# A hybrid HGRN2 / RWKV-7 backbone: small matmuls recorded in groups, HGRN2's key folded into its logarithms, and the mixers' weight remainders on VectorE

## The chip, the cores and the metric

The kernel runs on one core of one Trainium2 chip. The metric is the device time of one launch in microseconds; the kernel before took 4508.4 us (median of three runs, 4477.64 to 4508.42).

The names of a profile: PE is TensorE's matmuls and PEld its weight loads, DVE is VectorE, ACT is ScalarE, POOL is GpSimd, SP issues the DMAs.

## The reference

Four layers, each over 512 tokens (256 of context, 256 latent) of 1024 channels; in the last layer only the latent half is read out. A layer has a token mixer and a SwiGLU channel mixer. The token mixer feeds one input projection to two recurrences, merges them with sigmoid gates and projects out:

```python
p = modulate(rms_norm(x, g), shift, scale) @ w_in[l]          # 1024 -> 6528 columns
hg, rw, gates = split(p)
# HGRN2, per head of 128: forward and reversed, summed
S_t = diag(f_t) S_{t-1} + k_t v_t^T;   o_t = S_t^T q_t        # k = (1 - lb) sigmoid(-f)
# RWKV-7, per head of 64: forward and reversed, summed
S = S * w_t + (-S kk_t) b_t^T + v_t k_t^T;   y_t = S r_t
m = sigmoid(g_hg) * (o_hg @ proj_a) + sigmoid(g_rw) * (o_rw @ proj_b)
x = x + gate * rms_norm(m @ w_out)
x = x + gate * rms_norm((silu(h @ w1a) * (h @ w1b)) @ w2)     # 2816 hidden
```

## The kernel before

Everything is kept channel-major: 128 channels in the partitions, 512 tokens along the free axis. Each dense projection is done in three TensorE passes of rounded operands. A weight block of 512 rows by 128 columns comes by DMA into `wr`; ScalarE rounds it into `wh`; a subtraction gives the remainder `wl` (`load_split`); and a matmul each is made of `wh` with the rounded activations, `wh` with their remainder, and `wl` with the rounded ones (`mm3`). In a profile these are the `p_ps<-...` matmuls, 128 rows by 128 columns by 512 tokens. There are 102 such weight blocks in a layer's input projection.

The remainder's engine comes from `plan.lo(i)` and the table `LO`: entries 0 and 2 are for the input projections (layers 0 to 2, and the last), 1 and 3 for everything behind. A 1 stands for `plan.any`, VectorE or GpSimd, whichever the planner finds free first; a 0 for GpSimd.

The small matmuls are plain fp32, and each appears in a profile as two instructions:

- RWKV-7 works on four pairs of heads per layer. A pair holds head h = 0 in partitions 0 to 63 and head h = 1 in 64 to 127 (`hd[h]`). `rw_pair` builds the chunk products: `ZA` (64 x 64 blocks, `s_ps<-XS,BK` and `s_ps<-XS,X8b`, 64*64) and `SC` (64 rows to 128 columns, the same names, 64*128). `rw_solve` inverts the triangular blocks, mostly on VectorE. `rw_chain` goes through the eight chunks of 64 tokens and, at four of them, writes outputs (`c_ps<-SC,UV` with 128 rows, and `c_ps<-XS,S` with 64 rows in the half of the head).
- HGRN2 works on four heads per layer. `hg_head` makes the scores of a head level by level: at level h = 1, 2, 4, ..., 64 ScalarE takes exponentials of running sums of log forget gates (`PF`, `SB`, `SF`, `PB`) into X and Y, VectorE multiplies X by q and Y by the keys kf and kb, TensorE multiplies them (`score`, `g_ps<-hX,hY`), and GpSimd doubles the span of the sums.

These streams are recorded side by side, together with the projections of the gates. A list schedule (`Plan.schedule`) then gives each engine one fixed order: of what could start, what the longest chain of work hangs on. Its costs are a table in `Plan.cost`. `together()` records several instructions of an engine as one piece that nothing can come between. The engines run their lists in order; a wait at the head of a list holds all behind it. PSUM has four banks for projections (`p_ps`), two for `s_ps`, and one each for `c_ps` and `g_ps`.

The names are those of the line that issues everything (L341); a group is told by its tiles.

Of the kernel before, what the change touches and what calls it, by code (L numbers as in the profile page):

```python
# [10 lines left out]
F32R = mybir.dt.float32r  # L11
# [40 lines left out]
      ("X4c", 2, 1), ("SS", 2, 1), ("PF", 1, 2), ("SB", 1, 2), ("kf", 1, 2), ("kb", 1, 2))  # L52
# [9 lines left out]
LO = (1, 0, 1, 1)  # L62
ADA = (0.96, 0.58)
WRB, WSB = 4, 3
B2 = ("PF", "SB", "kf", "kb", "hq")
# [18 lines left out]
class Node:  # L84
    """One instruction, or several of an engine in a row, with what it waits for."""
# [7 lines left out]
class Plan:  # L93
    """Takes down the kernel's instructions, and emits them in the order of a list schedule: each engine runs, of what
    could start, what the longest chain of work hangs on."""
# [3 lines left out]
    def __init__(self, nc, tc):  # L99
        self.tc, self.nodes, self.tiles, self.tags, self.gang, self.kind = tc, [], {}, {}, None, None  # L100
        self.eng = dict(zip(self.ENG, (nc.tensor, nc.scalar, nc.vector, nc.gpsimd, nc.sync)))
# [22 lines left out]
    def region(a):  # L124
        """Partitions and elements that an access pattern spans."""
# [13 lines left out]
    def together(self):  # L139
        """The instructions recorded in this context, all of one engine, stay one after another."""  # L140
        @contextmanager
        def group():
            self.gang = -1
            yield
            self.gang = None
        return group()

    def add(self, engs, name, args, kw):
# [27 lines left out]
        costs = [self.cost(e, name, out, args, kw) for e in engs]  # L176
# [19 lines left out]
    def cost(eng, name, out, args, kw):  # L196
        """Nanoseconds that an instruction holds its engine."""
# [154 lines left out]
def body(ctx, tc, xT, cc, ada_w, w_in, rw_lo, rw_g2, proj_a, proj_b, w_out, ffn_w1, ffn_w2,  # L352
# [122 lines left out]
    def load_split(src, k0, nk, c0, ncol, place=None):  # L475
        """Weight rows k0*128.. and columns c0.. as its rounded part and the rest."""
# [24 lines left out]
    def psum2(w, src, hi, lo, rg=slice(0, T), tag="s"):  # L501
        """PSUM tile with w^T src for w of zeros and ones, src going in two parts."""
# [7 lines left out]
    def spots(tile):  # L510
        """Places for the split weights of one output tile in [P, 4, T]."""
# [7 lines left out]
    def proj(src, nk, c0, xh, xl, t0, place=None):  # L519
        """PSUM tile with W[:, c0:c0+128]^T x for tokens t0.., with a place for the weights stream by stream."""  # L520
# [24 lines left out]
    def norms(xs, t0, post=None, pre=None):  # L545
        """x += G * rms_norm(y), and then h = rms_norm(x) * A + B per channel and stream, split in two parts."""
# [79 lines left out]
    def ada_put(pm, b, n, ps):  # L626
        """Sums of n blocks of columns from b on, each stream's in 128 / 2 n rows, put channel-major in md."""
# [12 lines left out]
    def ada_first(l, pm):  # L640
        """The first four blocks of 512 columns of silu(c) @ ada_w[l], each in a quarter of the rows."""
# [14 lines left out]
    def ada_pair(l, pm, b):  # L656
        """Blocks b and b + 1, the products summed over the rows of each partition first."""
# [22 lines left out]
    def ada_finish(pm, i):  # L680
        """Scale, shift and gate of sub-layer i // 3 with the norm weights in."""
# [31 lines left out]
    def sigm(o, src, nb, t):  # L713
        """o = sigmoid(src - nb) by exp and ln; t is all of o."""
# [5 lines left out]
    def shifted(ps, j, lmu, t0, tag):  # L720
        """pf = p + mu (shift(p) - p) of projection tile j."""
# [20 lines left out]
    def layer(l, pm, xs, xd, hh, hl):  # L742
# [32 lines left out]
        def stacked(src, tags):  # L775
            """Per direction src's rounded part and the rest, in the two halves of the rows."""
# [33 lines left out]
        def rw_pair(p):  # L810
# [103 lines left out]
            if EA[last]:  # L914
                for d in range(2):
                    for h in range(2):
                        hs = hd[h]
                        ps = sps()
                        for i in range(NCH):
# [595 lines left out]
```

## Time and profile before

| | before |
|---|---|
| median of the runs | 4508.4 us (4477.64 to 4508.42) |
| span of the profiled execution | 4491.0 us |
| input projection and mixers of layers 0, 1, 2, 3 | about 630, 666, 665, 633 us |
| merge and channel mixer of layers 0, 1, 2, 3 | about 549, 505, 507, 276 us |

The profiled execution's span lies between the runs, 17.4 us below their median. The stages are told apart by their weight loads: the first loads of `w_in` lead the mixers, the first of `proj_a` the merge.

### The profile page before, as it was taken

To read this page: it belongs to the slowest core of one execution; us is meant where nothing else is said; L and a number is where in the kernel's file an instruction comes from. 1 tells how busy PE (TensorE), PEld (TensorE's weight loads), DVE (VectorE), ACT (ScalarE), POOL (GpSimd) and SP (SyncE) were. 2 spreads that over 40 slices of the span, in tenths; PEclk is the share of its full clock that TensorE was granted. 3 is DMA by queue.
4 is the path that set the end of the run, shared out by engine and by line. 5 is a ranking of instruction groups with operands and counts; after the bars stand their busy time and mean duration, and the time that the engine had idled before them with its cause. 6 is when DMAs were issued, how large, how long until landed. Compare 5 with 4: busy or idle time off the path is not lost. (4 is left out here: it accounts for less than half of the span.)

```text
span 4491.0 us, 72501 instructions
## 1 busy us (share of the span) xinstructions
PE 4151.3 (92%) x26290; PEld 3248.2 (72%) x26290; DVE 3314.2 (74%) x5772; ACT 2161.3 (48%) x4458; POOL 2318.9 (52%) x2121
## 2 busy tenths in 40 slices
PE   7999998899999999989999999999899989888998
PEld 5676776677777767778777676677777766667888
DVE  5988878977388898676627988876754487887665
ACT  4554653433255565534434554554433354554564
POOL 2464654465445456454654554554555535455542
PEclk8998899999998998899999998899999988887999
DMA  4211127455421111354433211116444421111555
GB/s 151 59 46 36 51 88 227 140 166 158 134 73 57 49 44 46 125 173 125 139 114 122 63 49 41 46 56 205 122 146 124 137 67 43 41 44 39 159 151 162
DMA packets 661415, 451.08 MB, mean 100 GB/s; under 512 B 28224, under 2 KB 584256, under 8 KB 661056
## 3 DMA queue, kind: packets, MB, share of 16 engines
q1 hardware_dynamic: 661056, 446.44, 33.1%
q8 instruction: 207, 3.39, 0.3%
q14 instruction: 152, 1.25, 0.1%
HBM read 416.98 MB, written 29.36 MB: 99 GB/s over the span
## 5 line engine op out<-in xcount | busy, mean ns | idle before, releaser
L341 POOL TENSOR_TENSOR wl<-wr,wh 128x512 fp32r<-128x512 f32 x726 | 1017.5, 1404 | 1034.3 <-ACT wh L341 705.9
L341 PE MATMUL p_ps<-hh,wh 128*128 128x512 f32 (+1 forms) x2784 | 1073.7, 398 | 30.2 <-ACT wh L341 15.8
L341 PE MATMUL p_ps<-hh,wl 128*128 128x512 f32 (+1 forms) x2784 | 1053.1, 397 | 30.9 <-POOL wl L341 21.4
L341 PE MATMUL p_ps<-hl,wh 128*128 128x512 f32 (+1 forms) x2784 | 1060.0, 394 | 0.0
L341 ACT ACTIVATE wh<-wr 128x512 fp32r<-128x512 f32 x986 | 610.0, 621 | 844.3 <-PE p_ps L341 678.8
L341 PEld LDWEIGHTS p_ps<-hh,wl 128*128 128x128 f32 x2784 | 544.5, 198 | 157.8 <-POOL wl L341 46.9
L341 PEld LDWEIGHTS p_ps<-hh,wh 128*128 128x128 f32 x2784 | 541.9, 197 | 145.2 <-ACT wh L341 26.9
L341 PEld LDWEIGHTS p_ps<-hl,wh 128*128 128x128 f32 x2784 | 543.4, 198 | 97.0 <-issue 9.2
L341 POOL TENSOR_SCALAR fn<-fn 128x512 f32<-128x512 f32 (+1 forms) x152 | 230.9, 1519 | 177.4 <-ACT fn L341 168.8
L341 DVE TENSOR_TENSOR fn<-fn,p_ps 128x512 f32<-128x512 f32 (+1 forms) x208 | 127.1, 614 | 219.9 <-ACT fn L341 129.0
L341 POOL TENSOR_SCALAR S0P<-S,pcs 128x64 f32<-128x64 f32 x192 | 156.7, 829 | 222.0 <-DVE S L341 221.2
L341 DVE TENSOR_TENSOR wl<-wr,wh 128x512 fp32r<-128x512 f32 x260 | 186.9, 723 | 101.1 <-ACT wh L341 59.7
L341 DVE TENSOR_TENSOR XS<-XS,S 64x30 f32<-64x30 f32 (+14 forms) x480 | 214.0, 446 | 10.8
L341 ACT ACTIVATE fn<-fn 128x512 f32<-128x512 f32 (+1 forms) x304 | 174.3, 574 | 89.7 <-POOL fn L341 84.9
L341 DVE TENSOR_TENSOR S<-XS 64x30 f32<-64x30 f32 (+14 forms) x480 | 207.3, 432 | 10.8
L341 PE MATMUL s_ps<-XS,X8b 64*64 64x64 f32 (+2 forms) x1024 | 147.2, 298 | 23.2 <-ACT X8a L341 14.5
L341 POOL TENSOR_TENSOR SF<-SF,PF 128x256 f32<-128x256 f32 x112 | 90.9, 812 | 139.0 <-ACT hY L341 138.2
L341 PEld LDWEIGHTS s_ps<-XS,X8b 64*128 64x128 f32 (+1 forms) x1024 | 118.9, 196 | 55.2 <-ACT X8a L341 24.1
L341 PE MATMUL s_ps<-XS,BK 64*64 64x64 f32 (+2 forms) x1024 | 139.2, 275 | 13.3 <-DVE XS L341 12.6
L341 PEld LDWEIGHTS s_ps<-XS,BK 64*128 64x128 f32 (+1 forms) x1024 | 107.9, 175 | 58.9 <-issue 37.1
L341 DVE SCALAR_TENSOR_TENSOR UV<-c_ps,pcs,S0P 64x64 f32<-64x64 f32 x384 | 108.6, 283 | 56.1 <-PE c_ps L341 45.6
L341 PE MATMUL p_ps<-SC,wh 128*128 128x512 f32 (+1 forms) x440 | 143.4, 363 | 2.4 <-ACT SC L341 2.2
(525 smaller groups left out, 9554.7 us busy)
## 6 DMA issues: line engine op xcount, KB each, us to landing
wr<-ffn_w SPq DMA_DIRECT2D x512, 256.0 KB, 3.0
wr<-w_in SPq DMA_DIRECT2D x408, 256.0 KB, 2.9
hq<-ada_w SPq DMA_DIRECT2D x242, 256.0 KB, 2.9
PB<-ada_w SPq DMA_DIRECT2D x110, 256.0 KB, 3.0
wr<-w_out SPq DMA_DIRECT2D x64, 256.0 KB, 3.0
gts<-fn SPq DMA_DIRECT2D x48, 256.0 KB, 3.0
wr<-proj_a SPq DMA_DIRECT2D x32, 256.0 KB, 4.5
wr<-proj_b SPq DMA_DIRECT2D x32, 256.0 KB, 3.8
```

What stands on the lines that cost most here:

```text
L341: getattr(self.eng[self.on[i]], name)(*args, **kw)
```

## The change

Three things are changed, none of which alters the amount of dense work.

**Small matmuls.** The `ZA` and `SC` products take two PSUM banks at a time, one for each head, and alternate between the heads, recorded with `together`. The outputs of the chain are sorted so that first all products with `UV` come, then all with the state `S`, alternating between the heads. The other small products of the chain are put in `together` as they are. The planner gets a smaller cost for such groups (`share`).

**HGRN2.** The exponential of the key's logarithm is no longer taken ahead; the logarithm is the start value of `SF` and `PB`. `SB` and `PF` lie in one tile `HA`, `SF` and `PB` in `HB`, and an access pattern (`both`) takes the two halves that a level needs in one instruction.

**Remainders.** `LO` goes from (1, 0, 1, 1) to (2, 0, 2, 1), where 2 is VectorE alone.

```diff
-LO = (1, 0, 1, 1)
+LO = (2, 0, 2, 1)
...
-        return self.any if LO[i] else self.pool
+        return self.vec if LO[i] == 2 else self.any if LO[i] else self.pool
...
+    def together(self, share=1.0):
         @contextmanager
         def group():
-            self.gang = -1
+            self.gang, self.share = -1, share
             yield
-            self.gang = None
+            self.gang, self.share = None, 1.0
...
-        costs = [self.cost(e, name, out, args, kw) for e in engs]
+        costs = [self.cost(e, name, out, args, kw) * self.share for e in engs]
...
+                    pz = [sps().rearrange("p (s c) -> p s c", s=4) for _ in range(2)]
+                    with plan.together(0.55):
+                        for i in range(4):
+                            for h in range(2):
+                                pe.matmul(pz[h][:, i, 0:w], BK[hd[h], s4 + i, :, :], ar[hd[h], s4 + i, 0:w // C, :],
+                                          start=True, stop=True)
                     for h in range(2):
-                        hs = hd[h]
-                        ps = sps()
-                        psv = ps.rearrange("p (s c) -> p s c", s=4)
-                        for i in range(4):
-                            pe.matmul(psv[:, i, 0:w], BK[hs, s4 + i, :, :], ar[hs, s4 + i, 0:w // C, :], start=True,
-                                      stop=True)
...
+                    steps += [(0, i, 0, n), (0, i, 1, sb)] + [(1, i, 0, n)] * (n > 0) + [(1, i, 1, sb)] * (sb > 0)
+                steps.sort()
+                fin = {i: x for x in steps for i in (x[1],)}
+                with plan.together(0.75):
+                    for x in steps:
+                        st_, i, d, n = x
+                        for h in range(2):
+                            po = ps[hd[h], 384 + i * C:384 + (i + 1) * C]
+                            if st_:
+                                w, a = S[hd[h], d, n % 4, :], ARt[hd[h], d, n, 1, :]
+                            else:
+                                w, a = UV[:, d, n, h, :], SC[:, d, n, h, C:P]
+                            pe.matmul(po, w, a[:, ::-1] if d else a, start=x == steps[0], stop=fin[i] == x,
+                                      skip_group_check=True)
...
-                act.activation(half(X, 0), half(SB, 0), AF.Exp)
-                act.activation(half(X, 1), half(PF, 1), AF.Exp)
-                act.activation(half(Y, 0), half(SF, 0), AF.Exp)
-                act.activation(half(Y, 1), half(PB, 1), AF.Exp)
+                def both(t, o, two, j=1):
+                    return bass.AP(t.tensor, t.offset + o, [t.ap[0], [2 * h, nb], [two, 2], [j, h]])
...
+                act.activation(pairs(X), both(HA, 0, T + h), AF.Exp)
+                act.activation(pairs(Y), both(HB, 0, T + h), AF.Exp)
                 vec.tensor_tensor(out=X, in0=X, in1=q, op=ALU.mult)
-                vec.tensor_tensor(out=half(Y, 0), in0=half(Y, 0), in1=half(kf, 0), op=ALU.mult)
-                vec.tensor_tensor(out=half(Y, 1), in0=half(Y, 1), in1=half(kb, 1), op=ALU.mult)
...
-                for dst, di, src, si, sj in ((SF, 0, PF, 1, h - 1), (PF, 1, PF, 0, h - 1),
-                                             (PB, 1, SB, 0, 0), (SB, 0, SB, 1, 0)):
-                    tot = half(src, si)[:, :, sj:sj + 1].to_broadcast([P, nb, h])
-                    pool.tensor_tensor(out=half(dst, di), in0=half(dst, di), in1=tot, op=ALU.add)
+                for t, o, two in ((HB, T + 2 * h - 1, 1 - T - 2 * h), (HA, h, T - 1)):
+                    r = both(t, 0, T + h)
+                    pool.tensor_tensor(out=r, in0=r, in1=both(HA, o, two, 0), op=ALU.add)
```

How the change moves instructions is seen at three places. On TensorE, at the `SC` products of the first pair of layer 1 (the rows `s_ps<-XS,...`; the `p_ps` rows are dense passes, `s_ps<-ident` transposes), before:

```order
L341 MATMUL s_ps<-XS,X8b 128x128
L341 MATMUL p_ps<-hh,wh 128x512
L341 MATMUL s_ps<-XS,X8b 128x128
L341 MATMUL p_ps<-hl,wh 128x512
L341 MATMUL s_ps<-XS,X8b 128x128 x2
L341 MATMUL s_ps<-ident,X4c 128x128 x2
L341 MATMUL p_ps<-hh,wl 128x512
L341 MATMUL p_ps<-hl,wh 128x512
L341 MATMUL p_ps<-hh,wl 128x512
L341 MATMUL c_ps<-UV,SC 64x64 x2
```

and in the changed kernel:

```order
L343 MATMUL s_ps<-XS,BK 128x128 x8
L343 MATMUL s_ps<-ident,BK 128x128 x4
L343 MATMUL s_ps<-ident,X4c 128x128 x2
L343 MATMUL c_ps<-UV,SC 64x64 x4
L343 MATMUL s_ps<-XS,X8b 128x128 x8
L343 MATMUL p_ps<-hh,wl 128x512
```

The `SC` products of 128 columns now stand in 56 rows of eight each; before, dense passes and other work split them into 202 rows. Over all of TensorE's list, a dense stretch is broken by something small 913 times, where it was 999.

On TensorE at the first outputs of layer 0, before and in the changed kernel:

```order
L341 MATMUL p_ps<-hh,wl 128x512 x2
L341 MATMUL c_ps<-SC,UV 64x64
L341 MATMUL c_ps<-XS,S 64x64 x2
L341 MATMUL c_ps<-SC,UV 64x64 x2
...
L341 MATMUL c_ps<-XS,S 64x64 x2
L341 MATMUL c_ps<-SC,UV 64x64
L341 MATMUL p_ps<-hh,wh 128x512
```

```order
L343 MATMUL p_ps<-hh,wl 128x512
L343 MATMUL c_ps<-SC,UV 64x64 x8
L343 MATMUL c_ps<-XS,S 64x64 x8
L343 MATMUL g_ps<-hX,hY 64x64 x8
L343 MATMUL c_ps<-UV,SC 64x64 x4
L343 MATMUL p_ps<-hh,wh 128x512
```

The eight switches between products of 128 and of 64 rows have become one. There are 56 such output groups in the program.

On GpSimd, at the first levels of the first HGRN2 head of layer 0, before and in the changed kernel:

```order
L341 TENSOR_TENSOR wl<-wr,wh 128x512
L341 TENSOR_SCALAR S0P<-S,pcs 128x64 x2
L341 TENSOR_TENSOR wl<-wr,wh 128x512
L341 TENSOR_SCALAR hq<-hq 128x512
L341 TENSOR_TENSOR PB<-PB,SB 128x128x2
L341 TENSOR_SCALAR S0P<-S,pcs 128x64 x2
L341 TENSOR_TENSOR SF<-SF,PF 128x128x2
L341 TENSOR_TENSOR SB<-SB 128x128x2
L341 TENSOR_TENSOR PF<-PF 128x128x2
```

```order
L343 TENSOR_TENSOR HB<-HB,HA 128x128x2x2
L343 TENSOR_TENSOR HA<-HA 128x128x2x2
L343 COPY pcs<-ep 128x8
L343 MEMSET ep 128x8
L343 TENSOR_SCALAR fn<-fn 128x512
L343 TENSOR_SCALAR S0P<-S,pcs 128x64 x2
L343 TENSOR_SCALAR hq<-hq 128x512
L343 TENSOR_TENSOR HB<-HB,HA 128x64x2x4
```

The remainders are gone from GpSimd's list here, and a level's four sums are two. Over the whole program 234 of the 705 remainders of 128 x 512 on GpSimd went to VectorE's list (252 there before, 486 now).

## Rows read from the trace of the kernel before

**Rows 1.** The page, parts 1 and 2: busy us (share) x instructions; the granted clock in slices.

```profile
PE 4151.3 (92%) x26290; PEld 3248.2 (72%) x26290; DVE 3314.2 (74%) x5772; ACT 2161.3 (48%) x4458; POOL 2318.9 (52%) x2121
...
PEclk8998899999998998899999998899999988887999
```

**Rows 2.** Busy us by stage: mixers of layers 0 to 3, one merge and channel mixer (1905:2410).

```profile
60.00:690.00 630.00, 595.70 (x4424) 448.54 (x4423) 528.63 (x1008) 352.19 (x757) 341.61 (x348) 0.92 0.20 61
...
1239.00:1905.00 666.00, 628.06 (x4552) 473.16 (x4552) 551.97 (x1057) 367.14 (x791) 351.36 (x358) 0.91 0.22 66
1905.00:2410.00 505.00, 483.71 (x2242) 390.69 (x2241) 289.92 (x382) 190.19 (x336) 278.50 (x202) 0.98 0.47 139
2410.00:3075.00 665.00, 624.53 (x4512) 468.48 (x4512) 550.34 (x1056) 365.97 (x788) 351.27 (x359) 0.91 0.22 66
...
3582.00:4215.00 633.00, 558.68 (x3983) 435.65 (x3982) 509.32 (x999) 334.65 (x772) 330.48 (x365) 0.83 0.20 58
```

**Rows 3.** Groups of instructions by form, TensorE's small products that the change regroups.

```profile
L341 PE MATMUL c_ps<-XS,S 64*64 64x64 f32 x800 | 96.6, 238 | 0.0
L341 PE MATMUL c_ps<-SC,UV 128*64 128x64 f32 x896 | 95.8, 252 | 13.9 <-DVE S L341 12.0 <-ACT UV L341 1.9
...
L341 PE MATMUL s_ps<-XS,X8b 64*128 64x128 f32 x448 | 93.7, 352 | 2.4 <-DVE SC L341 2.4
L341 PE MATMUL s_ps<-XS,BK 64*128 64x128 f32 x448 | 81.2, 303 | 0.7 <-ACT UV L341 0.5
...
L341 PE MATMUL s_ps<-XS,BK 64*64 64x64 f32 x512 | 46.9, 246 | 12.6 <-DVE XS L341 12.6
L341 PE MATMUL s_ps<-XS,X8b 64*64 64x64 f32 x512 | 39.3, 244 | 20.8 <-ACT X8a L341 14.5 <-DVE XS L341 6.1
```

**Rows 4.** Timeline of TensorE, layer 1: start us, us, what.

```profile
1334.97 0.27 PE L341 MATMUL s_ps<-XS,BK 64*128 64x128 f32 x1
1334.97 0.27 PE L341 MATMUL s_ps<-XS,X8b 64*128 64x128 f32 x1
```

**Rows 5.** Timeline of TensorE, layer 0.

```profile
253.19 0.45 PE L341 MATMUL c_ps<-S,AR 64*64 64x64 f32 x8
253.56 0.50 PE L341 MATMUL p_ps<-hl,wh 128*128 128x512 f32 x1
253.90 0.39 PE L341 MATMUL p_ps<-hh,wl 128*128 128x512 f32 x1
254.13 0.40 PE L341 MATMUL p_ps<-hh,wh 128*128 128x512 f32 x1
...
255.50 0.69 PE L341 MATMUL g_ps<-hX,hY 128*64 128x64 f32 x16
256.11 0.50 PE L341 MATMUL p_ps<-hh,wh 128*128 128x512 f32 x1
...
257.48 0.33 PE L341 MATMUL c_ps<-SC,UV 128*64 128x64 f32 x2
...
259.81 0.50 PE L341 MATMUL p_ps<-hh,wl 128*128 128x512 f32 x1
```

**Rows 6.** Groups by form on GpSimd and VectorE.

```profile
L341 POOL TENSOR_TENSOR wl<-wr,wh 128x512 fp32r<-128x512 f32 x705 | 1001.1, 1423 | 1013.4 <-ACT wh L341 685.0 <-PE p_ps L341 199.8 <-issue 44.0
L341 DVE TENSOR_TENSOR wl<-wr,wh 128x512 fp32r<-128x512 f32 x252 | 183.8, 732 | 100.2 <-ACT wh L341 58.8 <-PE p_ps L341 30.4 <-ACT UV L341 7.0
L341 POOL TENSOR_TENSOR PF<-PF 128x256 f32<-128x256 f32 x112 | 99.4, 887 | 4.4 <-ACT hX L341 3.6
L341 DVE TENSOR_TENSOR hY<-hY,kb 128x256 f32<-128x256 f32 x112 | 63.9, 571 | 0.6 <-ACT hY L341 0.2
```

**Rows 7.** One tile's instructions: duration ns minimum/median/maximum, first and last start.

```profile
L341 DVE TENSOR_TENSOR hX<-hX,hq x128: 673/684/2262, 143.6 to 4187.0; 128x512 f32<-128x512 f32 x128
```

**Rows 8.** Who waited for whom in layer 1's mixers: us in total, times, longest.

```profile
PE p_ps L341 <- DVE wl L341: 3.9, 2, 3.5
```

More of the change, by code (lines that the diff above doesn't have):

```diff
@@ L61 @@
 PN = (0, 0, 0, 0, 0, 0, 0, 0)
[L62 removed]
+LO = (2, 0, 2, 1)
 ADA = (0.96, 0.58)
 WRB, WSB = 4, 3
[L65 removed]
+B2 = ("HA", "HB", "hq")
 DMA_RATE = 300.0
@@ L934, in rw_pair @@
                     BK, ar = BKs[d], ARt[:, d]
-                    for h in range(2):
-                        hs = hd[h]
-                        ps = sps()
-                        psv = ps.rearrange("p (s c) -> p s c", s=4)
-                        for i in range(4):
-                            pe.matmul(psv[:, i, 0:w], BK[hs, s4 + i, :, :], ar[hs, s4 + i, 0:w // C, :], start=True,
-                                      stop=True)
+                    pz = [sps().rearrange("p (s c) -> p s c", s=4) for _ in range(2)]
+                    with plan.together(0.55):
+                        for i in range(4):
+                            for h in range(2):
+                                pe.matmul(pz[h][:, i, 0:w], BK[hd[h], s4 + i, :, :], ar[hd[h], s4 + i, 0:w // C, :],
+                                          start=True, stop=True)
+                    for h in range(2):
+                        hs, psv = hd[h], pz[h]
                         vec.tensor_tensor(out=SC[:, d, ss, h, 0:w], in0=psv[:, :, 0:w],
@@ L1042, in rw_chain @@
                 pu = ps[z0, 0:256]
-                for d in range(2):
-                    for h in range(2):
-                        pe.matmul(pu[:, (2 * d + h) * C:(2 * d + h + 1) * C], SC[:, d, s, h, 0:C], UV[:, d, s, h, :],
-                                  start=True, stop=True)
-                act.activation(Rs, pu, AF.Copy)
-                for d in range(2):
-                    for h in range(2):
-                        pe.matmul(ps[hd[h], d * C:(d + 1) * C], ZA[z0, d, s, h, :],
-                                  Rs[:, (2 * d + h) * C:(2 * d + h + 1) * C], start=True, stop=True)
+                with plan.together():
+                    for d in range(2):
+                        for h in range(2):
+                            pe.matmul(pu[:, (2 * d + h) * C:(2 * d + h + 1) * C], SC[:, d, s, h, 0:C],
+                                      UV[:, d, s, h, :], start=True, stop=True)
+                act.activation(Rs, pu, AF.Copy)
+                with plan.together():
+                    for d in range(2):
+                        for h in range(2):
+                            pe.matmul(ps[hd[h], d * C:(d + 1) * C], ZA[z0, d, s, h, :],
+                                      Rs[:, (2 * d + h) * C:(2 * d + h + 1) * C], start=True, stop=True)
                 for h in range(2):
@@ L1056, in rw_chain @@
                 if s < NCH - 1:
-                    for d in range(2):
-                        for h in range(2):
-                            pe.matmul(ps[hd[h], 256 + d * C:256 + (d + 1) * C],
-                                      BKT[:, d, s, h * C:(h + 1) * C], UV[:, d, s, h, :], start=True, stop=True)
+                    with plan.together():
+                        for d in range(2):
+                            for h in range(2):
+                                pe.matmul(ps[hd[h], 256 + d * C:256 + (d + 1) * C],
+                                          BKT[:, d, s, h * C:(h + 1) * C], UV[:, d, s, h, :], start=True, stop=True)
                     s0p = [None, None]
@@ L1130, in hg_head @@
             yield lambda: e < 2 or ("hg", e - 2) in flags
-            PF, SB = st("PF", [P, T]), st("SB", [P, T])
-            kf, kb = st("kf", [P, T]), st("kb", [P, T])
-            for d, lf, kx in ((0, PF, kf), (1, SB, kb)):
+            HA, HB = st("HA", [P, 2, T]), st("HB", [P, 2, T])
+            SB, PF = HA[:, 0, :], HA[:, 1, :]
+            SF, PB = HB[:, 0, :], HB[:, 1, :]
+            for d, lf, kx in ((0, PF, SF), (1, SB, PB)):
                 ci = d * 4 + e
@@ L1344, in layer @@
         mlb = st("X8b", [P, 4, T], F32R)
-        ml = [st(t, [P, T], F32R) for t in ("PF", "PF", "SB", "SB")] + [mlb[:, k, :] for k in range(4)]
+        ml = [t[:, i, :] for t in (st("HA", [P, 2, T], F32R), st("HA", [P, 2, T], F32R)) for i in range(2)]
+        ml += [mlb[:, k, :] for k in range(4)]
         xs = load_x(xd, t0)
```

41 lines of the change are left out of this document (15 added, 26 removed).

## The prediction

> **What bounds the kernel now.** I read the page's busy times first, then the stages, then the groups and the timeline of the stage that the change touches. TensorE is busy for 92% of the span and VectorE for 74% [rows 1], but these are averages over two kinds of stage. In merge and channel mixer (505 us in layer 1) TensorE is busy 484 us at a granted clock of 0.98 and VectorE only 290 us; the change leaves that work as it is, so I give those stages nothing. In the mixers of layers 0 to 2 TensorE is busy for 94% (628 of 666 us in layer 1) and VectorE for 83% (552); ScalarE and GpSimd have half their time free [rows 2]. So in some 1960 us of mixers TensorE is the bound, VectorE is next, and the granted clock of 0.91 to 0.92 is below that of the dense stages. The last layer's mixers are different: TensorE 559 of 633 us (88%), VectorE 509 (80%), clock 0.83. There no engine is full, and chains of waits take part of the time.
>
> **The change part by part.**
>
> Small matmuls. The `SC` products of 128 columns come to 93.7 + 81.2 = 175 us [rows 3]. Do two of them that use different halves of the rows run at once? The trace has a place where the order happened to put such two side by side: at 1334.97 us one with X8b and one with BK start together [rows 4]. So the changed order should halve these 175 us: -87; I take -80, for starts and ends of groups. The lower bound is nothing, if only the interleaving of two streams makes this possible. The `ZA` products come to 46.9 + 39.3 = 86 us [rows 3]; halved that is -43, and I take -40.
>
> Outputs. One group runs from 257.48 to 259.81, 2.33 us [rows 5]. What sixteen instructions cost that alternate between column halves without a switch is shown by the HGRN2 score: 255.50 to 256.11, 0.61 us [rows 5]. The changed group is two such blocks with one switch (about 0.15): 1.4 us. 56 groups save 0.95 us each, -53 us at that pace and -60 with the clock of these stages (0.91). Bounds: -30, if only the first half of a group gains, and -78, the halves of the two groups' busy times with something for the switches (192 us in all [rows 3], of which part overlaps).
>
> The Trainium skill (TensorEngine Tiling (Array Packing), Restrictions and Gotchas) says that different row tiles cannot use the same PSUM bank at once. Here the two heads of `SC` and `ZA` go to two banks, but the state half of an output group writes both heads into one `c_ps` bank. No row of before shows such a pair. By that rule the outputs would give about 30 us instead of 60, and the time would be 20 us above my forecast.
>
> Breaks. A dense pass follows the one ahead of it after 0.23 us (253.90 to 254.13), but takes 0.34 us behind a small group (253.56 to 253.90) [rows 5]; with the same at entry a break costs 0.2 to 0.25 us of dense time. 86 fewer breaks (999 to 913): -20 us.
>
> TensorE's sum is -80 - 40 - 60 - 20 = -200 us, 50 per layer; between -80 (no pairing of row halves) and -240.
>
> Remainders. 234 go from GpSimd at 1423 ns to VectorE at 732 ns [rows 6]: GpSimd -333, VectorE +171 us, about +43 per layer. HGRN2 takes away 224 products of the keys on VectorE at 571 ns [rows 6] (the twin with kf has the same count), -128, and 32 whole ones at the 684 ns of hX [rows 7], -22. VectorE's net is +21 us, 5 per layer. On GpSimd four sums of 887 ns become two of twice the size, for which the remainder's 1423 ns is the nearest row: 3.5 to 2.8 us, 112 times, -78. GpSimd's mixers fall from 351 us to about 250 per layer. That may help VectorE: hX takes 684 ns in the median and up to 2262 [rows 7], which is what an instruction with two SBUF inputs shows beside a busy GpSimd; I count 5 to 10 us per layer for it, which covers the +5. ScalarE's two large exponentials for four small ones save time on an engine that is half idle: nothing.
>
> What of it reaches the span. In layer 1 TensorE falls from 628 to 578 us and VectorE stays at about 552. If TensorE kept its 38 us of idle time, the stage would take 616 us, all 50 saved. But VectorE would then be at 90%, and the last layer shows that a stage in which TensorE isn't full has more idle time and a lower clock. Two thirds puts the stage at 633 us, TensorE at 91% and VectorE at 87%, between what layers 1 and 3 show. I take two thirds in every layer: 4 x 33 = -133 us. The profiled 4491 becomes 4358; the median stood 17 us above the span, so 4375 us. Late next is VectorE, and the chain from `SC` through its eviction to the state chain.
>
> **The rivals.**
>
> All of it arrives. TensorE stays the only bound and shorter small groups keep the clock up: -200 to -240, 4270 to 4310 us. For it speaks that TensorE's idle time in layers 0 to 2 is only about 5%.
>
> The row halves don't run together in the new order, because each fp32 product is two instructions with two weight loads and the two heads wait for each other's. Then outputs and breaks alone are left: two thirds of -80, 4455 us. Against it stands [rows 4].
>
> The clock takes it back. With less for TensorE to do its idle time grows, and the mixers of layers 0 to 2 fall to the 0.83 of the last layer's, where TensorE is 88% busy [rows 2]. 578 us of work at 0.91 is 634 at 0.83; with 38 idle that is 672 us, 6 more than now. Three such layers and a last one with -33: 4493 us, no change. Against it: cold stretches come with thin work as well as with gaps, and the change makes thin work denser. The Trainium skill (TensorE: Matmul & The Clock Gate, Why this matters for your kernels) says that idle gaps between bursts bring half the clock back, which is the rule behind this rival.
>
> Slower: the remainder waits in VectorE's queue. Before, the planner gave it to whichever engine was free; now 234 more stand in VectorE's list behind whatever is ahead of them, evictions and the solve's steps among them, and the `p_ps` pass that needs the remainder holds TensorE's whole list. Before, such waits were rare: 2 of them, 3.9 us in layer 1 [rows 8]. If each moved remainder holds TensorE for 1.0 us on average, one and a half of hX's 684 ns [rows 7], that is +234, and 234 - 133 = +101: 4609 us. It decides from 0.57 us on average, where it eats the gain; from 0.77 us the kernel is over 1% slower. Against it: a remainder is ready after 732 ns on VectorE, where GpSimd took 1423, and the weights are loaded ahead.
>
> **How the numbers follow.** A change under 1% (45 us) can't be told from none here: the runs of one kernel are 31 us apart. Forecast, between -90 and -195 us, 0.62. All of it, 0.10. No pairing of rows, 0.10, half of it within 1%. The clock, 0.09, within 1%, rarely beyond. The queue, 0.09, slower. Faster by over 1%: 0.62 + 0.10 + 0.05 = 0.77; slower: 0.10; within 1%: 0.13. The range goes from 4255 (TensorE's whole -240 and some clock) to 4500, and leaves the queue and a little on both sides out.
>
> **What would show it.** Right: mixers of layers 0 to 2 at about 630 us with TensorE at 91%; `SC` rows of sixteen instructions that take no longer than eight did, and groups of about 100 us instead of 175; output groups of some 1.4 us; 90 remainders per layer on VectorE, whose busy time hardly moves; GpSimd at 40% in these stages. Wrong: a `p_ps` wait for VectorE's `wl` of tens of microseconds per layer, a clock under 0.88 in the first three mixers, or paired `SC` instructions that start a full step apart. Merge and channel mixer should keep their 505 to 549 us; if they move by more than 10 us, the plan itself has shifted and my stages are no longer comparable.

## The result and the profile after

The changed kernel takes 4339.0 us in the median of four runs (4335.38 to 4342.33) against 4499.3 us of four runs of the kernel before beside them: a ratio of 0.965, interval 0.961 to 0.968, or -160 us where -133 was forecast. The profiled execution has a span of 4333.6 us (before 4491.0).

The page after, parts 1 and 2, answers to [rows 1]:

```profile
PE 3898.9 (90%) x26290; PEld 3081.4 (71%) x26290; DVE 3248.5 (75%) x5759; ACT 2147.8 (50%) x4234; POOL 1901.6 (44%) x1622
...
PEclk8999899999998998999999989889999997798999
```

TensorE is busy for 252 us less, and the span is 157 us shorter: 62% of it arrived. VectorE, which got 234 more remainders, is busy for 66 us less. GpSimd gave up 417 us. The mean granted clock is 0.925 (0.924 before).

The stages, as in [rows 2] (mixers of layers 0, 2 and 3, with layer 1's merge and channel mixer between):

```profile
60.00:654.00 594.00, 540.68 (x4403) 404.98 (x4403) 513.05 (x988) 347.38 (x697) 245.27 (x231) 0.92 0.21 61
...
1838.00:2346.00 508.00, 485.03 (x2264) 393.21 (x2263) 284.59 (x391) 193.52 (x341) 277.95 (x201) 0.98 0.48 143
2346.00:2980.00 634.00, 566.37 (x4494) 428.74 (x4494) 538.75 (x1042) 360.72 (x727) 245.40 (x237) 0.90 0.22 65
...
3489.00:4052.00 563.00, 478.03 (x3981) 384.83 (x3980) 485.19 (x995) 327.46 (x710) 224.93 (x234) 0.85 0.21 62
```

The mixers of layers 0, 2 and 3 lose 36, 31 and 70 us, those of layer 1 (not shown) 40; the dense stage between takes 508 us for 505. GpSimd stands at 225 to 249 us per layer (250 was forecast). In the last layer TensorE falls from 559 to 478 us.

TensorE's small products by form, as in [rows 3]:

```profile
L343 PE MATMUL s_ps<-XS,X8b 64*128 64x128 f32 x448 | 44.5, 344 | 1.2 <-DVE SC L343 0.8 <-DVE AR L343 0.4
L343 PE MATMUL c_ps<-SC,UV 128*64 128x64 f32 x896 | 40.4, 236 | 25.2 <-DVE S L343 24.9
L343 PE MATMUL c_ps<-XS,S 64*64 64x64 f32 x800 | 38.0, 236 | 0.0
L343 PE MATMUL s_ps<-XS,BK 64*128 64x128 f32 x448 | 35.6, 290 | 0.6 <-ACT UV L343 0.5
L343 PE MATMUL s_ps<-XS,BK 64*64 64x64 f32 x512 | 26.7, 277 | 19.1 <-DVE XS L343 18.8 <-DVE AR L343 0.2
L343 PE MATMUL s_ps<-XS,X8b 64*64 64x64 f32 x512 | 23.6, 249 | 12.0 <-DVE XS L343 12.0
```

One instruction still takes about as long as before (mean 236 to 344 ns), but the busy time of a group has fallen to between 39 and 60% of what it was. `SC` goes from 174.9 to 80.1 us, `ZA` from 86.2 to 50.3, the two rows of the outputs together from 192.4 to 78.4.

The timeline of TensorE, as in [rows 4, 5]. An `SC` row in layer 1, eight instructions of one head before and sixteen of both heads after:

```profile
1329.86 1.16 PE L341 MATMUL s_ps<-XS,X8b 64*128 64x128 f32 x8
```

```profile
1307.45 1.16 PE L343 MATMUL s_ps<-XS,BK 64*128 64x128 f32 x16
```

An output group of layer 0 after, of the kind that [rows 5] show before:

```profile
250.47 0.39 PE L343 MATMUL p_ps<-hl,wh 128*128 128x512 f32 x1
250.79 0.69 PE L343 MATMUL c_ps<-SC,UV 128*64 128x64 f32 x16
251.41 0.45 PE L343 MATMUL c_ps<-XS,S 64*64 64x64 f32 x8
251.79 0.50 PE L343 MATMUL p_ps<-hh,wl 128*128 128x512 f32 x1
```

It holds TensorE from 250.79 to 251.79, 1.0 us, where the group before took 2.33. But this is the small kind, of 24 instructions (12 of the 56 groups, where a chunk has no state yet). The other 44 have 32 instructions. One of them, before and after:

```profile
246.27 0.33 PE L341 MATMUL c_ps<-SC,UV 128*64 128x64 f32 x2 [0.50 <-DVE S L341]
...
249.07 0.79 PE L341 MATMUL p_ps<-hh,wh 128*128 128x512 f32 x1
```

```profile
511.16 0.69 PE L343 MATMUL c_ps<-SC,UV 128*64 128x64 f32 x16 [1.08 <-DVE S L343]
511.78 0.68 PE L343 MATMUL c_ps<-XS,S 64*64 64x64 f32 x16
512.39 0.49 PE L343 MATMUL g_ps<-nacc,vt 128*128 128x128 f32 x2
```

From the group's start to the next instruction that is 2.80 us before and 1.23 after, where the prediction said 1.4.

The remainders, HGRN2's sums and products, as in [rows 6, 7], by form and for one tile:

```profile
L343 POOL TENSOR_TENSOR wl<-wr,wh 128x512 fp32r<-128x512 f32 x471 | 657.1, 1398 | 675.5 <-ACT wh L343 480.9 <-PE p_ps L343 145.4 <-DMA hq<-ada_w 11.3
L343 DVE TENSOR_TENSOR wl<-wr,wh 128x512 fp32r<-128x512 f32 x486 | 361.9, 749 | 125.1 <-ACT wh L343 79.8 <-PE p_ps L343 25.9 <-ACT y L343 9.1
L343 POOL TENSOR_TENSOR HB<-HB,HA 128x512 f32<-128x512 f32 x112 | 162.6, 1452 | 113.9 <-ACT hY L343 110.6
L343 POOL TENSOR_TENSOR HA<-HA 128x512 f32<-128x512 f32 x112 | 144.4, 1289 | 19.7 <-ACT hX L343 14.0
```

```profile
L343 DVE TENSOR_TENSOR hX<-hX,hq x128: 652/688/1926, 152.1 to 4015.0; 128x512 f32<-128x512 f32 x128
```

And TensorE's waits (us in total, times, longest), in layer 1's mixers, as in [rows 8]:

```profile
PE p_ps L343 <- DVE wl L343: 14.3, 12, 5.3
PE c_ps L343 <- DVE S L343: 13.5, 10, 3.6
PE s_ps L343 <- DVE XS L343: 10.4, 6, 3.4
```

The wait for VectorE's remainders has grown from 3.9 to 14.3 us in this layer (over the program from 9.8 to 49.9). The rival's mechanism is there, at 0.17 us per moved remainder (40.1 us over 234) and not at one.

### The profile page after: what moved, and what is told of

It is laid out like the page before. It is cut to its first block, busy times and chain, and to the rows that moved or that the text cites. A ratio compares the mean times of both kernels' runs of the same rounds, so it can differ in the third digit from the quotient of the medians.

```text
span 4333.6 us, 71689 instructions
## 1 busy us (share of the span) xinstructions
PE 3898.9 (90%) x26290; PEld 3081.4 (71%) x26290; DVE 3248.5 (75%) x5759; ACT 2147.8 (50%) x4234; POOL 1901.6 (44%) x1622
## 4 chain that ended last, share of the span: by engine, by line
PE 40%; DVE 18%; issue 3%; ACT 2%; DMA 1%; POOL 1%; DVEq 0%; SPq 0%; POOLq 0%; ACTq 0%
PE p_ps L343 31%; PE s_ps L343 4%; DVE XS L343 3%; PE c_ps L343 3%; PE g_ps L343 2%; DVE wl L343 2%; DVE S L343 2%; DVE AR L343 1%; DVE hX L343 1%; DVE UV L343 1%; DVE X8b L343 1%; DVE X8a L343 1%; DVE fn L343 1%; DVE y L343 1%; DVE og L343 1%
## 5 line engine op out<-in xcount | busy, mean ns | idle before, releaser
L343 PE MATMUL p_ps<-hh,wh 128*128 128x512 f32 (+1 forms) x2784 | 1062.5, 393 | 35.7 <-ACT wh L343 24.4
L343 POOL TENSOR_TENSOR wl<-wr,wh 128x512 fp32r<-128x512 f32 x492 | 673.2, 1371 | 696.5 <-ACT wh L343 501.9
L343 DVE TENSOR_TENSOR wl<-wr,wh 128x512 fp32r<-128x512 f32 (+1 forms) x494 | 364.8, 743 | 126.0 <-ACT wh L343 80.8
L343 POOL COPY SC<-XS 64x256 f32<-64x256 f32 x128 | 73.6, 575 | 327.7 <-DVE SC L343 321.9
L343 POOL TENSOR_TENSOR HB<-HB,HA 128x512 f32<-128x512 f32 x112 | 162.6, 1452 | 113.9 <-ACT hY L343 110.6
L343 POOL TENSOR_TENSOR HA<-HA 128x512 f32<-128x512 f32 x112 | 144.4, 1289 | 19.7 <-ACT hX L343 14.0
L343 ACT ACTIVATE fn<-p_ps 128x512 f32<-128x512 f32 (+1 forms) x217 | 113.1, 521 | 50.9 <-PE p_ps L343 33.8
L343 POOL TENSOR_SCALAR X8a<-X8a 128x512 f32<-128x512 f32 x64 | 106.9, 1670 | 41.2 <-ACT X8a L343 38.7
```

The costliest lines, as they stand in the source:

```text
L343: getattr(self.eng[self.on[i]], name)(*args, **kw)
```

## The experiments

All runs in one table. Idle is the span less TensorE's busy time; busy times are of the pages.

| kernel | median us | ratio (interval) | span | TensorE busy | idle | VectorE | GpSimd |
|---|---|---|---|---|---|---|---|
| before | 4499.3 | 1 | 4491.0 | 4151.3 | 339.7 | 3314.2 | 2318.9 |
| after | 4339.0 | 0.965 (0.961 to 0.968) | 4333.6 | 3898.9 | 434.7 | 3248.5 | 1901.6 |
| groups alone | 4403.0 | 0.978 (0.976 to 0.981) | 4404.6 | 3903.7 | 500.9 | 3358.4 | 2314.7 |
| HGRN2 alone | 4489.0 | 0.997 (0.996 to 0.999) | 4475.2 | 4135.5 | 339.7 | 3220.7 | 2193.4 |
| LO alone | 4554.4 | 1.012 (1.008 to 1.016) | 4557.3 | 4193.2 | 364.1 | 3322.7 | 1974.4 |
| after, old LO | 4382.5 | 0.974 (0.971 to 0.977) | 4375.0 | 3903.0 | 472.0 | 3262.4 | 2185.3 |
| after, old HGRN2 | 4366.5 | 0.970 (0.967 to 0.972) | 4368.1 | 3891.0 | 477.1 | 3322.1 | 1999.2 |
| after, no groups | 4549.7 | 1.010 (1.007 to 1.013) | 4546.2 | 4164.6 | 381.6 | 3213.9 | 1887.8 |
| after, no alternation | 4437.5 | 0.986 (0.983 to 0.988) | 4435.5 | 4051.5 | 384.0 | 3247.9 | 1905.2 |
| after, lag 250 | 4353.4 | 0.967 (0.965 to 0.969) | 4353.0 | 3895.7 | 457.3 | 3259.5 | 1890.5 |
| after, old outputs | 4436.9 | 0.984 (0.982 to 0.986) | 4451.1 | 4002.3 | 448.8 | 3270.2 | 1900.2 |
| after, old SC and ZA | 4409.7 | 0.979 (0.977 to 0.980) | 4415.3 | 4040.6 | 374.7 | 3223.6 | 1865.4 |
| after, filler of sums | 4497.0 | 0.999 (0.997 to 1.001) | 4500.8 | 3952.7 | 548.1 | 3242.8 | 2703.2 |
| after, filler of memsets | 4431.4 | 0.984 (0.982 to 0.985) | 4427.2 | 3930.5 | 496.7 | 3223.6 | 2477.2 |

Below, differences between two kernels in us are differences of their ratios times 4500 us; the kernel before stood between 4499.3 and 4503.3 in all series.

### One part alone

The three parts, each put into the kernel before by itself. Groups:

```diff
+                    with plan.together(0.55):
+                        for i in range(4):
+                            for h in range(2):
...
+                with plan.together(0.75):
```

> The kernel before with the small-matmul groups alone (ZA, SC, outputs and the chain in groups; HGRN2 and LO as before). If TensorE is the bound of the mixers, nearly the whole gain is here: 4345 to 4390 us, TensorE's busy time in the mixers down by about 260 us, its idle time there up by 60 to 100. If VectorE stands right behind TensorE, so that the groups need the load that HGRN2's rewrite takes from VectorE, only half: 4410 to 4440 us.

Measured: -98 us, between the two ranges, with 248 us off TensorE's busy time and 161 us more of idle time. More than half of that growth stands in two of TensorE's waits in that kernel:

```profile
PE s_ps L343 <- DVE XS L343: 70.2, 23, 7.9
PE c_ps L343 <- DVE S L343: 64.0, 49, 4.4
```

Before, these two are 21.2 and 24.1 us. They are the solve and the state chain of RWKV-7: with the dense work shorter, it is VectorE's steps there that TensorE waits for.

HGRN2's sums and exponentials alone:

```diff
-                act.activation(kx, kx, AF.Exp)
...
+                act.activation(pairs(X), both(HA, 0, T + h), AF.Exp)
+                act.activation(pairs(Y), both(HB, 0, T + h), AF.Exp)
...
+                    pool.tensor_tensor(out=r, in0=r, in1=both(HA, o, two, 0), op=ALU.add)
```

> The kernel before with the HGRN2 rewrite alone. If TensorE is the bound, VectorE's 150 us and GpSimd's 80 us were not on the path: 4475 to 4505 us. If VectorE and GpSimd bound the mixers beside TensorE: 4420 to 4460 us.

Measured: -13 us. VectorE loses 94 us of work and GpSimd 126, and nearly none of it was on the path.

The remainders alone:

```diff
-LO = (1, 0, 1, 1)
+LO = (2, 0, 2, 1)
```

> The kernel before with the mixers' weight remainders on VectorE alone. VectorE gets 170 us more in the mixers and nothing is taken from it: if TensorE is the bound and waits for remainders are few, 4500 to 4530 us; if remainders queue in VectorE's list and hold TensorE, 4560 us or more; if a remainder that is ready 0.7 us earlier and a quieter GpSimd are worth something, 4450 to 4480 us.

Measured: +56 us, slower by 1.2%, between the ranges for few waits and for a queue. TensorE's busy time grows by 42 us at a lower clock (0.907 against 0.924) and its idle time by 24.

### The whole without one part

The changed kernel with `LO` as before:

```diff
-LO = (2, 0, 2, 1)
+LO = (1, 0, 1, 1)
```

> The changed kernel with LO back at (1, 0, 1, 1), so that VectorE or GpSimd takes a mixer's remainder. The trace after shows TensorE waiting 50 us for VectorE's remainders. If these waits are the price of the move: 4300 to 4330 us. If the move pays by a quieter GpSimd and quicker remainders: 4360 us or more. If it is neither: 4335 to 4350 us.

Measured: 41 us slower than the changed kernel. The same two numbers cost 56 us in the kernel before and give 41 here. The next two kernels ask which of the other parts turns it round. The changed kernel with HGRN2 as before:

```diff
+                act.activation(kx, kx, AF.Exp)
...
-                act.activation(pairs(X), both(HA, 0, T + h), AF.Exp)
-                act.activation(pairs(Y), both(HB, 0, T + h), AF.Exp)
```

> The changed kernel without the HGRN2 rewrite: groups and remainders on VectorE. If the remainders on VectorE pay only because HGRN2's rewrite has made room there, this is slower than the groups alone (4403 us): 4430 to 4470 us, VectorE over 88% in the mixers. If the rewrite of HGRN2 doesn't matter to it: 4350 to 4380 us.

And the changed kernel with all small products, their order and the planner's costs for them as before:

```diff
-                    with plan.together(0.55):
...
-                with plan.together(0.75):
```

> The changed kernel without the groups: HGRN2's rewrite and the remainders on VectorE. TensorE stays 94% busy in the mixers. If room on VectorE is what makes the remainders pay, this is at or below the rewrite alone (4489 us): 4450 to 4490 us. If the move of the remainders costs in itself (55 us, as measured alone) and the changed kernel's good result is another thing: 4520 to 4550 us.

Measured: 4366.5 and 4549.7 us. With the single parts this fills a table of what each part does in the company of the others, in us:

| | neither | with the first | with the second | with both |
|---|---|---|---|---|
| groups (with HGRN2, LO) | -98 | -106 | -191 | -204 |
| LO (with HGRN2, groups) | +56 | +58 | -38 | -41 |
| HGRN2 (with groups, LO) | -13 | -21 | -11 | -24 |

So it is the groups that decide the sign of `LO`, and HGRN2 has no part in it. The idea that the room which HGRN2 frees on VectorE makes the moved remainders pay has fallen: with HGRN2 and without groups they cost 58 us.

### What the groups give

The changed kernel with the two heads one after the other inside each group; the groups, their places and the planner's costs stay:

```diff
-                        for i in range(4):
-                            for h in range(2):
+                        for h in range(2):
+                            for i in range(4):
...
```

> The changed kernel with each group as it is, but the two heads of ZA, SC and the outputs one after the other inside the group instead of alternating; same order of everything else. If two row halves (or column halves) running at once is what the groups bring, TensorE's busy time in the mixers rises by some 130 to 170 us and the kernel takes 4420 to 4470 us; the SC group then takes 1.9 us at full clock instead of 1.1. If grouping (fewer breaks, fewer switches) is what brings the gain, it stays within 20 us of the changed kernel's 4339.

Measured: 94 us slower, TensorE busy 153 us longer. Its groups by form, and its output group on the timeline:

```profile
L343 PE MATMUL c_ps<-SC,UV 128*64 128x64 f32 x896 | 83.3, 242 | 24.8 <-DVE S L343 24.6
L343 PE MATMUL c_ps<-XS,S 64*64 64x64 f32 x800 | 77.2, 240 | 0.0
L343 PE MATMUL s_ps<-XS,X8b 64*128 64x128 f32 x448 | 63.2, 345 | 0.8 <-DVE SC L343 0.8
L343 PE MATMUL s_ps<-XS,BK 64*128 64x128 f32 x448 | 48.3, 285 | 0.0
```

```profile
256.75 0.68 PE L343 MATMUL c_ps<-SC,UV 128*64 128x64 f32 x8
257.36 0.44 PE L343 MATMUL c_ps<-XS,S 64*64 64x64 f32 x4
257.73 0.68 PE L343 MATMUL c_ps<-SC,UV 128*64 128x64 f32 x8
258.34 0.44 PE L343 MATMUL c_ps<-XS,S 64*64 64x64 f32 x4
258.71 0.50 PE L343 MATMUL p_ps<-hh,wl 128*128 128x512 f32 x1
```

The same 24 instructions take 1.96 us one head after the other and 1.0 us alternating (and 2.43 and 1.23 us where there are 32): pairing by heads is real, for `SC,UV` (different column halves) and for `XS,S` (different row and column halves, one PSUM bank) alike. The outputs stand at 160.5 us here, 78.4 with alternation, 192.4 before. For `SC` it is the other way round: 111.5 here, 80.1 with alternation, 174.9 before; of the 95 us the larger part, 63 us, comes from standing together, away from the dense passes, and 31 us from alternation. The split is rough: a row's busy time counts time in which another product runs beside it, too.

Outputs as before, all else changed:

```diff
-                with plan.together(0.75):
-                    for x in steps:
...
+                    for h in range(2):
...
+                        pe.matmul(po, UV[:, 0, n, h, :], SC[:, 0, n, h, C:P], start=True, stop=False)
...
```

> The changed kernel with the chain's outputs in the order and without the group of before; the SC and ZA pairs stay. The prediction put the outputs at 60 us of TensorE and two thirds of it in the time: 40 us, so 4379 us. If the state half of a group pairs too, although both heads write one PSUM bank, TensorE's busy time rises by 70 to 90 us and the time by 45 to 65, to 4384 to 4404 us. If only the UV half gains: 30 us of TensorE, 20 of the time, 4359 us.

Measured: 86 us slower, more than expected even if the state half pairs; TensorE busy 103 us longer, idle 14 us longer. Most of what the outputs save arrives, 86 of 103 us. They stand in the state chain itself: with the old ones the last product of the chain starts 15 to 30 us later in each of the four layers, and the last weight load of the input projection is issued 6 to 39 us later.

`SC` and `ZA` as before, all else changed:

```diff
-                    with plan.together(0.55):
+                    for h in range(2):
...
+                        ps = sps()
...
-                            for h in range(2):
```

> The changed kernel with the SC and ZA products head after head and without groups, as before; the outputs stay grouped. The prediction put SC at 80 and ZA at 40 us of TensorE, and two thirds in the time: 80 us, so 4419 us. If pairing is worth what it was sized at, TensorE's busy time rises by 110 to 130 us (with some breaks more) and the time by 70 to 95 us. Rival: the state chain that follows SC ends last in the changed kernel, so that SC's later end costs more than its TensorE time: over 110 us.

Measured: 64 us slower, less than expected, though TensorE is busy 142 us longer, more than expected; it is idle 60 us less. Under half of the larger saving arrives. The rival, a dearer late `SC`, is out: the chain's last product moves by only -3 to +8 us per layer, while the last load of the input projection comes 31 to 36 us later in layers 0 to 2 (8 in the last).

### The plan

A number of the planner that means nothing physical here, 10 ns on one lag:

```diff
-    LAG = dict(pe=dict(pe=0.0, act=240.0, vec=240.0,
+    LAG = dict(pe=dict(pe=0.0, act=250.0, vec=240.0,
```

> The changed kernel with one number of the planner's table shifted (the lag from TensorE to ScalarE 250 instead of 240 ns): the same instructions in another order. If differences of 20 to 50 us between the kernels are mechanisms, this stays within 15 us of 4339. If the order that the planner happens to find is worth that much by itself, it moves by 20 to 60 us, and single differences of that size prove nothing.

Measured: 9 us slower. This one new order is worth so much by itself; more of them were not tried. The groups' and `LO`'s effects are four times that and more; HGRN2's 11 to 24 us, and the difference between 38 and 41, are not to be read closely.

### What moving the remainders does

In the pair of the changed kernel and the one with the old `LO`, VectorE has 275 and 494 remainders (eight of them of 256 columns), +162 us, and yet its busy time is 14 us shorter with the 494. In the other three pairs of the table it moves by +8, -36 and -7 us. So its other instructions have become faster, by about what the remainders cost. These are two of them in the kernel with the old `LO`, and in the changed one:

```profile
L343 DVE TENSOR_TENSOR S<-XS 64x30 f32<-64x30 f32 (+14 forms) x480 | 242.2, 505 | 11.9
L343 DVE TENSOR_TENSOR XS<-XS,S 64x30 f32<-64x30 f32 (+14 forms) x480 | 226.8, 472 | 11.8
```

```profile
L343 DVE TENSOR_TENSOR XS<-XS,S 64x30 f32<-64x30 f32 (+14 forms) x480 | 208.2, 434 | 11.3
L343 DVE TENSOR_TENSOR S<-XS 64x30 f32<-64x30 f32 (+14 forms) x480 | 198.7, 414 | 11.1
```

They are the steps of the solve. The timeline of the kernel with the old `LO` shows one, of VectorE and of GpSimd:

```profile
153.49 1.35 DVE L343 TENSOR_TENSOR S<-XS 64x228 f32<-64x228 f32 x1
...
155.60 0.39 DVE L343 TENSOR_TENSOR XS<-XS,S 64x228 f32<-64x228 f32 x1
```

```profile
153.30 1.29 POOL L343 TENSOR_TENSOR wl<-wr,wh 128x512 fp32r<-128x512 f32 x1 [5.53 <-ACT wh L343]
155.63 0.62 POOL L343 COPY SC<-XS 64x256 f32<-64x256 f32 x1 [1.04 <-DVE SC L343]
```

The step that starts 0.19 us behind a remainder on GpSimd ends 0.25 us after it, 1.35 us long; the next of the same size, beside a copy, takes 0.39. I matched each of the 480 `S<-XS` with the GpSimd instruction that it overlaps longest: with the old `LO`, 105 lie beside a `wl`, `HA` or `HB` of 512 columns and take 1.06 us in the mean, the other 375 take 0.35; in the changed kernel 46 and 434, 1.10 and 0.34 us.

Is it any work of GpSimd with two inputs, or any work at all? Two kernels leave the changed order as it is and put extra work for GpSimd behind each of the mixers' remainders, on a small tile of its own, for which nobody waits. There are 408 such places, since the marking took in the remainders that VectorE had before too; the load put back is 802 and 576 us, more than the 284 that `LO` takes away.

```diff
+                if i in self.beside:
+                    for _ in range(5):
+                        g.tensor_tensor(out=z, in0=z, in1=z, op=ALU.subtract)
```

> The changed kernel with its order on every engine as it is; behind each of the 234 moved remainders' places GpSimd gets five extra subtractions of 128 x 64 on a tile of their own (about 1.4 us together, two inputs each), which nobody waits for. Theory: VectorE's own instructions take longer while GpSimd works on two inputs, and moving the remainders pays because that load goes away; between the changed kernel and the one with the old LO, VectorE's instructions other than wl come to some 150 us less at about equal counts, the solve's S<-XS and XS<-XS,S ahead of all (242 to 199 and 227 to 208 us). Then the extra load brings VectorE's busy time up by 80 to 150 us, S<-XS back to 225 to 245 us, and the time from 4339 to 4360 to 4385 us. Rival: what pays is only that a remainder is ready after 0.7 us and not after 1.4. Then VectorE's busy time stays within 20 us, and the time rises by at most 10 us.

```diff
+                if i in self.beside:
+                    for _ in range(10):
+                        g.memset(z, 0.0)
```

> As the run with extra subtractions, but the extra work on GpSimd at each place is ten memsets of 128 x 64, about as long together, which only write. Theory: it is GpSimd's reading of two inputs that slows VectorE; memsets leave VectorE's busy time within 30 us, and the time rises by 0 to 15 us, for GpSimd's own instructions that stand behind them. Rival: GpSimd's queue alone matters (its state products and sums come later): then this run and the one with subtractions rise alike. Second rival: any GpSimd work slows VectorE; then VectorE's busy time rises alike in both.

Measured: +155 and +86 us over the changed kernel, far more than either side expected, and VectorE's busy time 6 and 25 us shorter. The theory as put has failed in its size: extra work with two inputs on GpSimd doesn't bring VectorE's busy time up. The groups in the kernel with the subtractions:

```profile
L345 DVE TENSOR_TENSOR S<-XS 64x30 f32<-64x30 f32 (+14 forms) x480 | 193.8, 404 | 11.1
...
L348 POOL TENSOR_TENSOR dum<-dum 128x64 f32<-128x64 f32 x2040 | 859.2, 421 | 145.3
```

With these short instructions `S<-XS` keeps its 0.4 us (the 199 beside a filler take 0.36). In direction the theory holds: against steps of the same size beside nothing, 54 of the 199 are longer by over 0.02 us, the longest by 0.13, and none of the 166 beside a memset is. The subtraction is held, too: it takes 0.29 us beside nothing or beside a VectorE `tensor_tensor` that reads PSUM, and 0.52 in the mean beside one that reads SBUF alone. It is the long GpSimd instructions, 1.3 to 1.45 us, whose end a VectorE step waits for at a price that counts. The Trainium skill (SBUF — State Buffer, SBUF: two separate sides) says that a VectorE instruction with two SBUF inputs and a GpSimd one that reads SBUF hold a shared pair of ports as a lock, whoever starts first for the whole instruction. The 1.35 us above and the subtractions' two lengths agree; that a step loses at most 0.13 us beside a subtraction shows how little a short holder costs. What the fillers cost instead is GpSimd's own queue, as far as the waits tell. ScalarE's there:

```profile
ACT X8a L345 <- POOL X8a L345: 78.8, 39, 5.0
ACT hX L345 <- POOL HA L345: 60.0, 42, 5.7
ACT hY L345 <- POOL HB L345: 44.6, 25, 5.2
```

In the changed kernel they are 13.1, 1.3 and 9.2 us. In the chain that ended last GpSimd stands at 12 and 9% of the span with the fillers, where it had 1%. TensorE is idle for 113 and 62 us longer, and busy for 54 and 32 us longer at a granted clock of 0.910 and 0.918. The order doesn't know of the fillers, so these prices (155 of 802, 86 of 576) are those of unplanned load. An estimate from them: at 0.15 to 0.19 us per us, the 284 us that `LO` takes off GpSimd would be worth 42 to 55 us, as much as its whole gain.

What do the remainders decide, then? Counted from a layer's first load of `w_in`, its last load of `w_in` is issued and the last product of its state chain (`c_ps`) starts after so many us, in layers 0, 1, 2 and 3:

| | last load of `w_in` | last product of the chain |
|---|---|---|
| before | 642, 652, 652, 613 | 645, 656, 656, 631 |
| LO alone | 678, 669, 700, 595 | 655, 647, 673, 614 |
| groups alone | 626, 621, 626, 569 | 649, 648, 636, 582 |
| after, old LO | 602, 621, 623, 549 | 622, 643, 646, 584 |
| after | 609, 617, 622, 558 | 621, 627, 637, 570 |

The kernel before is balanced: the two ends lie 3 to 4 us apart in layers 0 to 2. The groups take 16 to 31 us from the dense work of these layers, and from the chain 8 and 20 us in two of them and nothing in layer 0: the chain now ends last. Among the groups and HGRN2's rewrite, `LO` brings the chain forward by 1, 16, 9 and 14 us and moves the dense work by +7, -4, -1 and +9. Alone, it sends the dense work of layers 0 to 2 back by 36, 17 and 48 us, and the chain comes forward in layer 1 only. In the last layer, where TensorE was not full before either, `LO` alone brings both forward, by 18 and 17 us. So it costs where the dense work bounds a layer and pays where the chain ends last. Taking the later of the two ends in each layer and adding the four up, `LO` gives -40 us in the changed kernel and +73 alone, where the times say -41 and +56; with the groups and the old HGRN2 it gives -48, with HGRN2's rewrite and no groups +59, where they say -38 and +58. That is read from the timelines of single executions; no run sets the two ends apart by itself.

## Why the prediction was right, point by point

**The bound.** TensorE in the mixers, with the dense stages untouched: held. Merge and channel mixer moved by 2 to 9 us per layer.

**TensorE's sum.** It was put at -200 us, -240 at most (the upper bounds of its terms add up to about -230), and is -252. By the rows, `SC` is -95 (-80 forecast) and `ZA` -36 (-40). With the old scores put back TensorE is busy 142 us longer (120 forecast for the two), with the old outputs 103 (60 forecast): the outputs are the term that was mis-sized. Their mechanism was right, and the 1.4 us of the changed group nearly so (1.23). The step that failed is the reading of the group before: the 2.33 us of [rows 5] are a group of 24 instructions, while the 1.4 us were built for 32, and 44 of the 56 groups have 32 and took 2.80 us at full clock where nothing stood between. By these rows they save 1.57 us each and the small ones 1.33, not 0.95; over 56 groups that would be 85 us at full clock.

The Trainium skill (TensorEngine Tiling (Array Packing), Restrictions and Gotchas) says that different row tiles cannot use one PSUM bank at once; by it the outputs would have given 30 us. Here the rows go the other way for products that differ in the column half as well: `XS,S`, both heads in one `c_ps` bank, takes 77.2 us head after head and 38.0 alternating. The pairing of `SC` was reasoned from one chance pair [rows 4]. It is right, but the run without alternation shows it to be the smaller part of that term, 31 of 95 us; most of the rest came from standing together, which the prediction had not counted there. That -80 was nearly met is in part luck.

**What of it arrives.** Two thirds were forecast, 62% came. The reason given was that VectorE and the chain from `SC` to the state chain come late next, and the waits of the kernel with the groups alone stand at VectorE's steps of the solve and the state chain. But the share is no constant. By layer the mixers gave back 65, 59, 53 and 87% of what TensorE lost there: the last layer, which the prediction took for its sign that less comes through where TensorE isn't full, let the most through and gave 70 us where 33 were forecast. By kernel the groups' share is 35% alone (86 of 248 us of span), 43% with HGRN2, 63% with `LO`, 80% with both; and the outputs pay most of their saving where `SC` and `ZA` pay under half. The flat two thirds lay between these by luck as much as by reason. There is luck in the sum, too: the -133 us were forecast for the groups, which alone give -98; the rest of the -160 is HGRN2 (-21 beside the groups) and `LO` (-41 beside both), which were put at about nothing.

**The remainders.** VectorE's net was put at +21 us and is -66. Adding the parts one after another, the groups bring +44 (no term of the sum), HGRN2 -96 (-150 forecast) and the remainders -14 (+171 forecast). GpSimd's 250 us per layer was met (HGRN2's sums gave 68 us of the 78: of the four only `PF` took 887 ns before, the others 803 to 846). The step that failed here is the worth of GpSimd's relief: "5 to 10 us per layer" through VectorE. VectorE's other work gave back some 176 us (162 + 14), four times the most of that. The forecast thus had the gain of `LO` at about nothing, where it is -41 us among the groups.

**The rivals.** All of it arriving is out (62%). The row halves pair. The clock held: 0.925 (0.924 before), with 0.85 to 0.92 in the mixers, though TensorE's idle time rose by 95 us; in the last layer it is 0.85 with TensorE 85% busy, where 0.83 stood beside 88%. The Trainium skill (TensorE: Matmul & The Clock Gate, Why this matters for your kernels) says that idle gaps between bursts bring half the clock back; by the mean clock, the added idle time did not do so here. Of the slower rival (which by its own numbers is over 1% slower from 0.76 us on, not 0.77) the sign came true where the groups are missing (+56 us), but not by its mechanism: the wait for VectorE's `wl` grows by 15 us there (9.8 to 24.7), and TensorE's 42 us at a lower clock carry more of it.

**Left open.** Why the moved remainders send the dense work back and lower the clock in the kernels without groups (0.907 and 0.917) wasn't found. And no run put instructions of 512 columns back on GpSimd with VectorE's list unchanged, so how `LO`'s 41 us divide between VectorE's faster steps and GpSimd's shorter queue isn't settled. That the long GpSimd instructions hold VectorE up is read from which instructions overlap, not from a run that changes them alone.

## What to carry to other kernels

Small matmuls of two heads in different halves of the array pay when they alternate and when they stand together, and here most where they lie on the chain that ends last: count those at nearly their full saving, and the rest at what the next engine leaves. A change that costs time by itself can pay beside another, so edits that meet on one engine are tried in both companies. An engine at 44% isn't free: look who waits for it in order, and what its long instructions hold up on its neighbour.

## What was not expected of the hardware

A VectorE instruction of two SBUF inputs that meets a GpSimd one of 128 x 512 with two inputs mostly lasts until that one's end (1.06 us in the mean instead of 0.35, 105 of 480), while GpSimd instructions of 128 x 64 with two inputs leave it at 0.36. With 219 remainders more, VectorE's busy time was 14 us shorter.

Products that share a PSUM bank but neither row nor column half run two at a time (eight `XS,S` of two heads within 0.45 us, four of one head within 0.44). On GpSimd a memset of 128 x 64 takes 0.15 us; a subtraction of that size takes 0.29 us undisturbed and 0.42 in the mean.
